# Smaller weight pieces, kept split parts and four row tiles in each sum over experts: a two-layer hybrid decoder trunk

## The chip, the cores and the metric

The kernel runs on one core of a Trainium2 chip. The core has five engines with instruction streams of their own: TensorE (PE, matrix multiplications into PSUM), VectorE (DVE), ScalarE (ACT), GpSimd (POOL) and SyncE (SP), which here issues every DMA. The metric is the time of the device in microseconds (us); lower is better. One execution was taken by the hardware profiler, and all rows of the trace come from it.

## The reference

Two layers over 1040 tokens (16 meta tokens and 1024 real ones; 112 padding places are masked) of width 1024, in float32. Each layer mixes tokens and then applies a product-key expert network:

```
for i in range(DEPTH):                                   # 2
    h = h + hybrid_mixer(rms_norm(h, attn_norm[i]), w_in[i], ..., w_out[i])
    h = h + peer_ffn(rms_norm(h, ffn_norm[i]), peer_w_q[i], peer_sub_keys[i], peer_u[i], peer_v[i])
return rms_norm(h[:, BLOCK:], final_norm)

# peer_ffn: 8 heads, 64 x 64 = 4096 experts, 16 chosen for each head
q = (xt @ wq).reshape(t, 8, 2, 128)
s = einsum('thpd,hpnd->thpn', q, sub_keys)               # scores of the two halves of a key
...                                                      # top 16 of the pairs, softmax g, expert idx
h_all = xt @ u.T                                         # (tokens, 4096): the hidden rows
a = gelu(take_along_axis(h_all, idx)) * g
w = zeros((t, 4096)).at[..., idx].add(a)
out = w @ v                                              # the sum over experts
```

The mixer projects the tokens to some 2300 columns, runs a sliding window attention, a stick-breaking attention and a gated linear attention on them, norms the three, and multiplies by `w_out`.

## The kernel before, in words

Activations are held transposed, 8 row tiles of 128 (`KT`) by tokens, and the tokens are cut in four quarters of 272, 256, 256 and 256 columns. The residual stream lies in DRAM.

**High and low parts.** A float32 product is made of three products in a rounded format, float32r: each operand is split into a high part (rounded, by ACT) and a low part (the difference, by DVE or POOL), and PE computes high x high, high x low and low x high. For weights, `wtile` loads 128x1024 float32 into one of three buffers `wraw`, and `split` (L273, L280) writes `whi` and `wlo`, two buffers each. `split_on` sets which engine takes the low part: POOL alone, or POOL and DVE a half each. For the weights of the sum over experts the other operand, `G`, is split too, for each row of experts r: `ah` on ACT (L1179), `al` on DVE (L1180).

**Stages of a layer.**
- Mixer: for each quarter 18 weight tiles of projections (`proj_span`) and 8 of the output (`out_span`), each through `dense` (L309 to L316): one tile, 8 x 3 matmuls over the quarter's columns. Every weight tile is loaded and split again in each quarter. The attention of a quarter is interleaved with the projections of the next one. `make_m` folds the query weights and keys into matrices `m`, which go to DRAM, 8 tiles of 128x1024 in each layer.
- Experts, for the first two quarters (P) and then for the last two (Q): `scores` multiplies the normed tokens by `m`, one head pair c at a time; `route` (many small DVE operations) finds the top 16; `hidden` runs over 32 row tiles r of u, each with 8 x 3 matmuls, and writes gelu of the result to `G`; `gates` builds the gate of every expert for 16 tokens at a time and multiplies it in; `values` sums over r = 0 to 31 with v, some row tiles d of the output at a time, accumulating in PSUM banks.
- In layer 0, the quarters of P are 272 and 256 columns wide, and a matmul takes one of them; in layer 1 the meta tokens are left out of P, both are 256 wide, and one matmul takes 512 columns. Q is 512 wide in both layers. `values` for P in layer 0 makes passes of 3, 3 and 2 row tiles (two banks for each row tile, six banks in all), and for P in layer 1 and Q in layer 0 two passes of 4. In the last layer, Q is summed in four passes: each quarter, row tiles 0 to 3, then each quarter, row tiles 4 to 7, with the final norm of P's quarters between the first two.
- During `values` of P the work of Q's first steps is spread over the loop: two `apply`, four `scores` (one after each 24 units of nd, from L1304 on), and the steps of `route`, `BUD * nd` of their estimated us after each r.

**Order.** The program is written as a stream of tile operations; a planner with a simulated timeline orders each engine's instructions, and each engine then runs its own in order, waiting on semaphores. SP too: a DMA that waits holds up those behind it.

Of the kernel before, what the change touches and what calls it, by code (L numbers as in the profile page):

```python
# [12 lines left out]
F32 = mybir.dt.float32  # L13
F32R = mybir.dt.float32r
# [28 lines left out]
class Span:  # L43
    """Token columns c0..c1 with their matmul chunks and 128-token tiles."""
# [18 lines left out]
def tile_trunk(ctx, tc, h0, w_pk, wgate, w2, glab, w_out, wqT, keysT, u_pk, v_w, sinks,  # L63
# [8 lines left out]
    # Buffers are views of two tiles, at fixed places: those of the mixer and of the experts share the room.  # L72
    # One tile has the operands rounded to float32r, the other the rest.
# [23 lines left out]
    g0 = lay(1, [("wraw", 1024, 3), ("ht", 528, 3), ("nsq", 528, 1), ("ndg", 128, 2), ("acc", T, 1), ("nms", 8, 2),  # L97
# [74 lines left out]
    set_rings(d=(0, 1), o=(2,), a=(3, 4, 5, 6, 7), h=(0, 1, 6, 7), g=(2, 3), v=(4, 5, 6, 7, 2, 3))  # L172

    # ---------------------------------------------------------------- constants
# [63 lines left out]
    # residual stream, transposed, in DRAM; sums of squares of each version on chip  # L238
# [25 lines left out]
    # ---------------------------------------------------------------- helpers  # L264
# [17 lines left out]
    def wload(src, n=1024):  # L282
        raw = sb([128, n], F32, "wraw", 4)
        SP.dma_start(raw, src)
        return raw

    def wtile(src, n=1024):
        raw = wload(src, n)
        n = raw.shape[1]
        hi = sb([128, n], F32R, "whi", 3)  # L290
        lo = sb([128, n], F32R, "wlo", 3)
        split(raw, hi, lo)
        return hi, lo

    class Rows:
        """Row tiles of hi and lo parts, in two halves."""
# [12 lines left out]
    def dense(wsrc, x, sp, xo=0):  # L309
        wh, wl = wtile(wsrc)  # L310
        ps = ps1("d")[:, 0:sp.w]
        for k in range(KT):
            ks = slice(k * 128, (k + 1) * 128)
# [5 lines left out]
    def rstd(ver, sp, sqk=None):  # L319
        """Reciprocal root mean square of each token of a quarter, on every partition."""  # L320
# [27 lines left out]
    def apply(ver, sp, g, x, rb, ks=range(KT), src=None):  # L348
        """Normed rows of a quarter, hi and lo."""
# [11 lines left out]
    # ---------------------------------------------------------------- folded product keys  # L361
    m_scr = [[dram.tile([128, KT * 128], F32, name=f"m{l}_{i}", tag=f"m{l}_{i}") for i in range(8)]
             for l in range(DEPTH)]

    def make_m(l, i):
        wq = [wload(wqT[l, 2 * i + e]) for e in range(2)]
        kt = sb([128, 2, 64], F32, "kt", 2)
        SP.dma_start(kt, keysT[l][:, 2 * i:2 * i + 2, :])
        for half in range(2):
            ps = ps1("d")  # L370
            for e in range(2):
                PE.matmul(ps[64 * e:64 * e + 64, :], kt[:, e, :], wq[e][:, half * 512:half * 512 + 512],
                          start=True, stop=True)
# [7 lines left out]
            SP.dma_start(m_scr[l][i][:, half * 512:half * 512 + 512], mk)  # L381

    # ---------------------------------------------------------------- attention
# [20 lines left out]
    def proj_span(l, L, sp, x):  # L404
        """Projections of a span: two blocks, with the meta tokens before them in the first."""
# [5 lines left out]
        def proj(g):  # L411
            return dense(w_pk[l, g], x, sp)
# [46 lines left out]
        # gate: hi and lo parts of the 16 columns stacked on 32 output rows  # L459
# [30 lines left out]
    def gla_setup(l, L, A):  # L490
# [4 lines left out]
        # GLA factors over the two blocks of the span; every exponent is at most zero  # L495
# [45 lines left out]
    def post(l, A, src, k0, nk, b0, nb, m, t0, gate=False, scale=1.0, eps=None):  # L541
        """Per-head norm, gain or gate of rows k0.. of the mix: src [128, (block, row tile, token)]; hi and lo parts."""
# [38 lines left out]
    def swa(l, L, A, n):  # L581
        """Sliding window of block n (-1: the meta tokens): query rows, keys of this block and the one before."""
# [8 lines left out]
        for kh in range(2):  # L591
# [34 lines left out]
            # the sum of the exponentials only scales its row, which the norm takes out but for its epsilon  # L626
# [29 lines left out]
    def sbreak(l, L, A, n, oT):  # L656
        """Stick breaking of block n: product of (1 - beta) over the newer keys, times beta."""
# [15 lines left out]
        for p in range(2):  # L673
            carry = [None, None]
            om = None
            for ci in range(nch):
# [4 lines left out]
                for e in range(2):  # L681
# [7 lines left out]
                    # t = tanh(z / 2): beta = (1 + t) / 2, 1 - beta = (1 - t) / 2  # L689
# [54 lines left out]
    def gla(l, L, A, n, outp=True):  # L744
        """Gated linear attention of block n: chunks of 8 directly, rectangles between them, state before."""
# [670 lines left out]
```

## Time and profile before

| | |
|---|---|
| median of 3 runs | 3486.05 us (3485.88 to 3488.12) |
| profiled execution, span from first to last instruction | 3482.2 us; a time of its own is not listed, and the span is 3.85 us under the median |
| mean granted TensorE clock | 0.956 of full speed |
| busy: PE, DVE, POOL, ACT | 3189.6, 2656.3, 1658.7, 1506.9 us |
| DMA | 373.16 MB, mean 107 GB/s |

Busy times overlap: each engine has its own. A stage's length less PE's busy time in it is the time in which PE had nothing to multiply. In the rows below, "x" is a count, "<-" in a group's tail names what ended the idle time before it, and L280 is line 280 of the kernel.

### The profile page before, as it was taken

How to read it: one execution, taken by the hardware profiler on the slowest of the kernel's cores; microseconds unless marked ns; L12 is line 12 of the kernel's file. 1: busy time of each engine (PE TensorE's matmuls, PEld its weight loads, DVE VectorE, ACT ScalarE, POOL GpSimd, SP SyncE). 2: the span in 40 equal slices, each digit the busy share in tenths (PEclk: the TensorE clock that was granted, in tenths of full speed). 3: DMA queues.
4: the chain of work that ended last, by engine and by line, in shares of the span. 5: the costliest groups of instructions: out<-in, count | busy, mean ns of one | idle time of the engine just before them, and what ended most of it. 6: DMA issues, size and time to landing. Idle time of an engine off the chain costs nothing. (4 is left out here: it accounts for less than half of the span.)

```text
span 3482.2 us, 62244 instructions
## 1 busy us (share of the span) xinstructions
PE 3189.6 (92%) x22843; PEld 2680.2 (77%) x22843; DVE 2656.3 (76%) x7223; ACT 1506.9 (43%) x3181; POOL 1658.7 (48%) x1179
## 2 busy tenths in 40 slices
PE   8999999988889988999899999999879899989899
PEld 7677887688879877887776878876768677767798
DVE  4667667599896799786356676676899868988887
ACT  4555545432234444334344545454323333333465
POOL 4435454343484433574432454543435534446655
PEclk9899998999899999999999999999989999999999
DMA  5434442342113322223433353333422133322454
GB/s 151 132 96 160 117 127 81 116 143 68 56 47 101 97 87 76 79 73 101 133 102 128 104 166 115 117 103 114 149 73 66 62 108 118 105 71 73 126 188 160
DMA packets 180948, 373.16 MB, mean 107 GB/s; under 512 B 18257, under 2 KB 79777, under 8 KB 180641
## 3 DMA queue, kind: packets, MB, share of 16 engines
q1 hardware_dynamic: 180640, 369.18, 33.7%
q8 instruction: 179, 2.93, 0.3%
q14 instruction: 129, 1.05, 0.1%
HBM read 341.71 MB, written 27.39 MB: 106 GB/s over the span
## 5 line engine op out<-in xcount | busy, mean ns | idle before, releaser
L280 POOL TENSOR_TENSOR arena_r<-arena,arena_r 128x512 fp32r<-128x512 f32 (+2 forms) x540 | 1108.1, 2053 | 1266.5 <-ACT arena_r L273 1217.4
L273 ACT ACTIVATE arena_r<-arena 128x1024 fp32r<-128x1024 f32 (+1 forms) x550 | 574.6, 1045 | 719.0 <-issue 207.3
L1186 PE MATMUL b<-arena_r 128*128 128x256 f32 (+2 forms) x4608 | 774.0, 326 | 73.1 <-DVE arena_r L1180 61.6
L1086 PE MATMUL b<-arena_r 128*128 128x512 f32 (+2 forms) x3840 | 792.4, 366 | 35.8 <-ACT arena_r L273 21.9
L1186 PEld LDWEIGHTS b<-arena_r 128*128 128x128 f32 x4608 | 667.4, 192 | 173.7 <-DVE arena_r L1180 94.5
L1086 PEld LDWEIGHTS b<-arena_r 128*128 128x128 f32 x3840 | 649.6, 199 | 141.4 <-ACT arena_r L273 24.9
L315 PE MATMUL b<-arena_r 128*128 128x256 f32 (+1 forms) x4992 | 696.0, 294 | 25.6 <-DVE arena L337 4.9
L315 PEld LDWEIGHTS b<-arena_r 128*128 128x128 f32 x4992 | 639.6, 195 | 62.1 <-issue 25.4
L1180 DVE TENSOR_TENSOR arena_r<-arena,arena_r 128x256 fp32r<-128x256 f32 (+2 forms) x448 | 399.9, 912 | 120.9 <-ACT arena_r L1179 119.5
L280 DVE TENSOR_TENSOR arena_r<-arena,arena_r 128x512 fp32r<-128x512 f32 (+1 forms) x290 | 234.7, 809 | 259.3 <-ACT arena_r L273 256.6
L1179 ACT ACTIVATE arena_r<-arena 128x256 fp32r<-128x256 f32 (+2 forms) x448 | 208.2, 474 | 170.4 <-PE b L1186 154.0
L1124 DVE TENSOR_TENSOR arena<-arena 128x2048 f16<-128x2048 f16 x129 | 200.3, 1555 | 40.0 <-PE b L1141 40.0
L1159 POOL TENSOR_TENSOR arena<-arena 128x352 f32<-128x352 f32 (+21 forms) x129 | 156.8, 1227 | 63.8 <-DVE arena L1147 34.7
L966 PE MATMUL b<-arena_r 128*128 128x256 f32 (+1 forms) x544 | 159.0, 295 | 16.3 <-POOL arena_r L280 9.4
L967 PE MATMUL b<-arena_r 128*128 128x256 f32 (+1 forms) x544 | 158.2, 294 | 7.8 <-DVE arena_r L359 7.8
L965 PE MATMUL b<-arena_r 128*128 128x256 f32 (+1 forms) x544 | 154.7, 293 | 2.6 <-ACT arena_r L358 1.1
L696 DVE TENSOR_TENSOR_SCAN arena<-arena,zf 128x272 f32<-128x272 f32 (+6 forms) x116 | 120.5, 1045 | 32.5 <-ACT arena L691 31.6
L256 POOL TENSOR_TENSOR arena<-arena 128x256 f32<-128x256 f32 (+2 forms) x105 | 99.8, 950 | 81.9 <-ACT arena L255 81.8
L1128 DVE TENSOR_TENSOR arena<-arena 128x512 f16<-128x512 f16 x129 | 127.4, 988 | 8.1 <-PE b L1153 7.8
L1146 ACT ACTIVATE arena<-b 128x64 f32<-128x64 f32 (+27 forms) x256 | 62.8, 283 | 160.5 <-DVE arena L1147 130.2
L1093 POOL TENSOR_TENSOR arena<-arena 128x272 f32<-128x272 f32 (+25 forms) x86 | 96.1, 1122 | 75.6 <-DVE arena L1147 48.0
L1129 DVE TENSOR_TENSOR arena<-arena 128x512 f16<-128x512 f16 x129 | 129.6, 1005 | 0.0
(277 smaller groups left out, 4613.7 us busy)
## 6 DMA issues: line engine op xcount, KB each, us to landing
arena<-in_w_pk_dram SPq DMA_DIRECT2D x144, 512.0 KB, 3.6
arena<-in_v_w_dram SPq DMA_DIRECT2D x136, 512.0 KB, 3.4
arena<-in_u_pk_dram SPq DMA_DIRECT2D x128, 512.0 KB, 3.5
arena<-in_w_out_dram SPq DMA_DIRECT2D x64, 512.0 KB, 3.7
arena<-m SPq DMA_DIRECT2D x92, 256.0 KB, 3.5
arena<-h SPq DMA_DIRECT2D x136, 128.0 KB, 2.3
arena<-in_wqT_dram SPq DMA_DIRECT2D x32, 512.0 KB, 3.8
arena<-in_v_w_dram SPq DMA_DIRECT2D x32, 384.0 KB, 3.1
```

Source lines behind the costliest of these rows:

```text
L273: ACT.activation(hi, src, AF.Copy)
L280: e.tensor_tensor(lo[:, a:b], src[:, a:b], hi[:, a:b].bitcast(F32), op=ALU.subtract)
L315: PE.matmul(ps, wt[:, ks], x.at(low, k, xo, sp.w), start=(k == 0 and i == 0), stop=(k == KT - 1 and i == 2))
L965: PE.matmul(ps[0:m, 0:256], yv(half, 0, k, oo, m), mh, start=(k == 0), stop=False)
L966: PE.matmul(ps[0:m, 0:256], yv(half, 0, k, oo, m), ml, start=False, stop=False)
L967: PE.matmul(ps[0:m, 0:256], yv(half, 1, k, oo, m), mh, start=False, stop=(k == KT - 1))
L1086: PE.matmul(ps, wt[:, ks], yv(h, low, k, 0, w // 2 if h is None else w), start=(k == 0 and i == 0), stop=(k == KT - 1 and i == 2))
L1124: DVE.tensor_tensor(Lh, iotaM.unsqueeze(1).to_broadcast([128, 4, 128, 4]), v4(P.mT, 128), op=ALU.is_equal)
L1159: POOL.tensor_tensor(G[:, 0:n, t0:t0 + 16], gt[:, 0:n], G[:, 0:n, t0:t0 + 16], op=ALU.mult)
L1179: ACT.activation(ah, G[:, r, o:o + w], AF.Copy)
L1180: last = DVE.tensor_tensor(al, G[:, r, o:o + w], ah.bitcast(F32), op=ALU.subtract)
L1186: PE.matmul(ps, wt[:, co:co + 128], pr[low], start=(r == 0 and i == 0), stop=(r == 31 and i == 2))
```

## The change

A weight piece is now 128x512: `wraw` has four buffers of 512, `whi` and `wlo` five each. At its first use a piece is split and, under a key, its low part (and for the projections and the output its high part too) is stored in DRAM. At later uses of the same key the low part is loaded from there; the high part is loaded too where it was kept, and converted again from the loaded weights where it was not. Keys: the projections and outputs of all four quarters, the scores' matrices (halves of P, and Q), u and v for P and Q. `values` always takes four row tiles at a time; where the two quarters are not merged, the second one's sums lie two to a bank. In the last layer Q's first four row tiles are summed for both quarters at once; the other four, a quarter at a time, under no key. `m` is stored as four matrices of 128x2048 per layer, one for each head pair, and `scores` puts two token tiles in one bank. `make_m` loads halves.

```diff
-    r0 = lay(0, [("whi", 1024, 2), ("wlo", 1024, 2), ("ah", 272, 4), ("al", 272, 4)], 0)
+    r0 = lay(0, [("whi", 512, 5), ("wlo", 512, 5), ("ah", 272, 4), ("al", 272, 4)], 0)
...
-    g0 = lay(1, [("wraw", 1024, 3), ("ht", 528, 3), ("nsq", 528, 1), ("ndg", 128, 2), ("acc", T, 1), ("nms", 8, 2),
+    g0 = lay(1, [("wraw", 512, 4), ("ht", 528, 3), ("nsq", 528, 1), ("ndg", 128, 2), ("acc", T, 1), ("nms", 8, 2),
...
+    kept = {}
+    def keep(name, part):
+        t = dram.tile([128, 512], F32, name=name, tag=name)
+        SP.dma_start(t, part.bitcast(F32))
+        return t
+    def wpiece(src, key=None, both=False):
+        hi = sb([128, 512], F32R, "whi")
+        lo = sb([128, 512], F32R, "wlo")
+        if key not in kept:
+            split(wload(src), hi, lo)
+            if key is not None:
+                kept[key] = (keep(f"{key}h", hi) if both else None, keep(f"{key}l", lo))
+            return hi, lo
+        kh, kl = kept[key]
+        if kh is None:
+            ACT.activation(hi, wload(src), AF.Copy)
+        else:
+            SP.dma_start(hi.bitcast(F32), kh)
+        SP.dma_start(lo.bitcast(F32), kl)
+        return hi, lo
...
-    def dense(wsrc, x, sp, xo=0):
-        wh, wl = wtile(wsrc)
+    def dense(wsrc, x, sp, key, xo=0):
...
+            if k % 4 == 0:
+                wh, wl = wpiece(wsrc[:, k * 128:(k + 4) * 128], f"{key}_{k // 4}", True)
...
     def scores(l, P, c, halves, ring):
+        pairs = [own[i:i + 2] for i in range(0, len(own), 2)]
+        bks = [ps1(ring) for _ in pairs]
+        for kq in range(4):
+            wh, wl = wpiece(m_scr[l][c][:, kq * 512:(kq + 1) * 512], f"m{l}_{c}_{kq}")
...
     def hidden(l, P, G, lo, hi, ring, cst=None, end=32):
-            wh, wl = wtile(u_pk[l, r])
...
+                if k % 4 == 0:
+                    wh, wl = wpiece(u_pk[l, r][:, k * 128:(k + 4) * 128], f"u{l}_{r}_{k // 4}")
...
-    def values_steps(l, P, G, halves, d0, nd, hs=None):
+    def values_steps(l, P, G, halves, d0, hs=None, reuse=True):
...
+        for i, (h, o, w) in enumerate(cs):
+            for d in range(4):
+                if i and d % 2:
+                    accs[d][i] = (bank[:, 256:256 + w], False, True)
+                else:
+                    bank = ps1("v")
+                    accs[d][i] = (bank[:, 0:w], True, not i)
+        for r in range(32):
+            wh, wl = wpiece(v_w[l][:, r, d0 * 128:d0 * 128 + 512], f"v{l}_{r}_{d0}" if reuse else None)
...
-        for d, nd in ((0, 4), (4, 4)) if P.merge else ((0, 3), (3, 3), (6, 2)):
-            for last, whole in values_steps(l, P, G, (0, 1), d, nd):
+        for d in (0, 4):
+            for last in values_steps(l, P, G, (0, 1), d):
...
-                if whole and work and step >= EVERY:
+                if work and step >= EVERY:
...
-                    left = BUD * nd
+                    left = BUD * 4
...
-        values(l, Q, G, (0,), 0, 4, hs)
+        values(l, Q, G, (0, 1), 0, hs)
...
-        values(l, Q, G, (1,), 0, 4, hs)
         for half, (o, sp) in enumerate(Q.parts):
-            values(l, Q, G, (half,), 4, 4, hs)
+            values(l, Q, G, (half,), 4, hs, False)
```

## Rows read from the trace of the kernel before

**Rows 1.** The page's part 1: busy us (share of the span) x instructions.

```profile
PE 3189.6 (92%) x22843; PEld 2680.2 (77%) x22843; DVE 2656.3 (76%) x7223; ACT 1506.9 (43%) x3181; POOL 1658.7 (48%) x1179
```

**Rows 2.** Stretches: start:end, length; PE, PEld, DVE, ACT, POOL busy; clock; DMA share, GB/s.

```profile
100.00:640.00 540.00, 517.34 (x3893) 398.34 (x3892) 364.98 (x738) 284.16 (x666) 250.03 (x225) 0.95 0.39 123
1050.00:1350.00 300.00, 264.65 (x2013) 254.32 (x2012) 249.61 (x1030) 135.21 (x291) 118.96 (x65) 0.97 0.30 93
1350.00:1595.00 245.00, 231.09 (x1346) 186.83 (x1347) 208.01 (x413) 92.17 (x239) 149.38 (x102) 0.96 0.25 78
1850.00:2440.00 590.00, 567.50 (x4246) 443.05 (x4245) 403.49 (x862) 306.33 (x687) 257.34 (x230) 0.96 0.39 123
2500.00:2770.00 270.00, 233.50 (x1812) 187.93 (x1810) 255.99 (x742) 84.39 (x159) 140.04 (x80) 0.93 0.22 69
2770.00:3030.00 260.00, 235.94 (x1153) 188.28 (x1154) 206.41 (x842) 92.83 (x141) 102.27 (x43) 0.99 0.33 106
3030.00:3265.00 235.00, 218.59 (x1292) 177.35 (x1291) 209.24 (x455) 87.39 (x227) 144.14 (x89) 0.96 0.25 79
3265.00:3482.00 217.00, 198.77 (x1631) 195.73 (x1629) 174.71 (x242) 119.06 (x213) 123.92 (x67) 0.96 0.55 175
```

**Rows 3.** The timeline, PE: start us, length us, line, operation, shape, count.

```profile
1799.78 34.47 PE L1186 MATMUL b<-arena_r 128*128 128x512 f32 x146
3338.24 27.03 PE L1186 MATMUL b<-arena_r 128*128 128x256 f32 x228
```

**Rows 4.** The timeline around 2803 us: DVE and POOL.

```profile
2800.35 0.69 DVE L1180 TENSOR_TENSOR arena_r<-arena,arena_r 128x512 fp32r<-128x512 f32 x1
2803.11 2.41 POOL L280 TENSOR_TENSOR arena_r<-arena,arena_r 128x1024 fp32r<-128x1024 f32 x1 [4.05 <-ACT arena_r L273]
2803.59 3.08 DVE L1180 TENSOR_TENSOR arena_r<-arena,arena_r 128x512 fp32r<-128x512 f32 x2 [2.55 <-ACT arena_r L1179]
```

**Rows 5.** Groups by shape, DVE and ACT: busy us, mean ns | idle before.

```profile
L1180 DVE TENSOR_TENSOR arena_r<-arena,arena_r 128x512 fp32r<-128x512 f32 x128 | 157.1, 1237 | 77.4 <-ACT arena_r L1179 76.5
L1179 ACT ACTIVATE arena_r<-arena 128x512 fp32r<-128x512 f32 x128 | 79.5, 622 | 78.5 <-PE b L1186 77.9 <-POOL arena L1159 0.6
L273 ACT ACTIVATE arena_r<-arena 128x1024 fp32r<-128x1024 f32 x518 | 547.6, 1058 | 694.9 <-issue 201.5 <-PE b L1186 173.7 <-PE b L315 107.2
```

**Rows 6.** Waits of PE, whole span: us in total, times, longest us.

```profile
PE b L1186 <- DVE arena_r L1180: 61.6, 71, 2.4
PE b L1110 <- DVE arena L1019: 19.1, 2, 12.4
```

**Rows 7.** POOL's splits: the page's group, then the 512-column shape alone.

```profile
L280 POOL TENSOR_TENSOR arena_r<-arena,arena_r 128x512 fp32r<-128x512 f32 (+2 forms) x540 | 1108.1, 2053 | 1266.5 <-ACT arena_r L273 1217.4
L280 POOL TENSOR_TENSOR arena_r<-arena,arena_r 128x512 fp32r<-128x512 f32 x280 | 467.9, 1672 | 513.9 <-ACT arena_r L273 484.6 <-issue 26.8 <-DMA arena<-h 2.4
```

**Rows 8.** The stretch 1050 to 1350, L1180 alone: DVE busy us (count).

```profile
1050.00:1350.00 300.00, 127.04 (x185) 0.97 0.30 93
```

**Rows 9.** Groups by shape, 1350 to 1595 us: PE's gate matmuls.

```profile
L1141 PE MATMUL b<-arena 128*128 128x64 f16 x512 | 35.7, 242 | 2.0 <-DVE arena L1147 2.0
```

**Rows 10.** DMA issues: count, KB each, median us from issue to landing.

```profile
arena<-m SPq DMA_DIRECT2D x92, 256.0 KB, 3.5
arena<-in_w_pk_dram SPq DMA_DIRECT2D x144, 512.0 KB, 3.6
```

**Rows 11.** Waits of SP, whole span: us in total, times, longest us.

```profile
SPq L354 <- DVE arena_r L359: 100.6, 50, 7.7
SPq L246 <- DMA h<-arena: 83.7, 49, 4.1
SPq L261 <- DVE arena L260: 64.8, 37, 8.5
```

**Rows 12.** Stretches of the first quarters' projections, columns as in rows 2.

```profile
25.00:100.00 75.00, 66.02 (x485) 60.18 (x484) 35.58 (x91) 36.35 (x81) 33.76 (x30) 0.95 0.46 138
1675.00:1760.00 85.00, 74.37 (x502) 67.78 (x502) 25.70 (x39) 30.42 (x47) 38.36 (x22) 0.98 0.46 144
```

More of the change, by code (lines that the diff above doesn't have):

```diff
@@ L370, in make_m @@
             ps = ps1("d")
+            wq = [wload(wqT[l, 2 * i + e][:, half * 512:half * 512 + 512]) for e in range(2)]
             for e in range(2):
-                PE.matmul(ps[64 * e:64 * e + 64, :], kt[:, e, :], wq[e][:, half * 512:half * 512 + 512],
-                          start=True, stop=True)
+                PE.matmul(ps[64 * e:64 * e + 64, :], kt[:, e, :], wq[e], start=True, stop=True)
             mt = sb([128, 512], F32, "ht")
@@ L952, in scores @@
[L952 removed]
         if P.s[c] is None:
[L954 removed]
+            P.s[c] = sb([128, P.ns, len(sp.tiles), 4, 64], F32, "s")[:, c % P.ns]
             if sp.meta:
                 POOL.memset(P.s[c][:, 0], 0.0)
[L957 to L968 removed]
+        own = [(j, o, m) for j, (o, m) in enumerate(sp.tiles) if (1 if o >= P.parts[1][0] else 0) in halves]
@@ new lines, in scores @@
+        own.sort(key=lambda t: -t[2])
+        pairs = [own[i:i + 2] for i in range(0, len(own), 2)]
+        bks = [ps1(ring) for _ in pairs]
+        for kq in range(4):
+            wh, wl = wpiece(m_scr[l][c][:, kq * 512:(kq + 1) * 512], f"m{l}_{c}_{kq}")
+            for bk, pair in zip(bks, pairs):
+                for e, (j, o, m) in enumerate(pair):
+                    half = 1 if o >= P.parts[1][0] else 0
+                    oo = o - P.parts[half][0]
+                    ps = bk[0:m, e * 256:e * 256 + 256]
+                    for kk in range(2):
+                        k = 2 * kq + kk
+                        for i, (low, wt) in enumerate(((0, wh), (0, wl), (1, wh))):
+                            PE.matmul(ps, yv(half, low, k, oo, m), wt[:, kk * 256:kk * 256 + 256],
+                                      start=(k == 0 and i == 0 and e == 0),
+                                      stop=(k == KT - 1 and i == 2 and e == len(pair) - 1))
@@ L970, in route @@
+        for bk, pair in zip(bks, pairs):
+            for e, (j, o, m) in enumerate(pair):
+                ACT.activation(P.s[c][0:m, j], bk[0:m, e * 256:e * 256 + 256].rearrange("p (a n) -> p a n", a=4), AF.Copy)
     def route(*args):
@@ new lines, in values_steps @@
+        accs = [[None] * len(cs) for d in range(4)]
+        for i, (h, o, w) in enumerate(cs):
[7 more added lines that the diff above has]
+            wh, wl = wpiece(v_w[l][:, r, d0 * 128:d0 * 128 + 512], f"v{l}_{r}_{d0}" if reuse else None)
+            parts = []
+            for h, o, w in cs:
+                tg = "2" if w > 272 else ""
+                ah = sb([128, w], F32R, "ah" + tg)
+                al = sb([128, w], F32R, "al" + tg)
+                ACT.activation(ah, G[:, r, o:o + w], AF.Copy)
+                last = DVE.tensor_tensor(al, G[:, r, o:o + w], ah.bitcast(F32), op=ALU.subtract)
+                parts.append((ah, al))
+            for d in range(4):
+                for i, (wt, low) in enumerate(((wh, 0), (wh, 1), (wl, 0))):
+                    for (ps, opens, closes), pr in zip(accs[d], parts):
+                        PE.matmul(ps, wt[:, d * 128:d * 128 + 128], pr[low], start=(opens and r == 0 and i == 0),
+                                  stop=(closes and r == 31 and i == 2))
+            yield last.ins
@@ L1191, in values_steps @@
+        for d in range(4):
+            for (ps, _, _), (h, o, w) in zip(accs[d], cs):
                 sp = P.sp if h is None else P.parts[h][1]
```

85 lines of the change are left out of this document (17 added, 68 removed).

## The prediction

> **What bounds the kernel now.** I read the page first: TensorE (PE) is busy 92% of 3482.2 us, VectorE (DVE) 76, GpSimd (POOL) 48 and ScalarE (ACT) 43% [rows 1]. So work that leaves ACT, POOL and DVE is worth only what it now costs PE in waits. The stretches by stage come next [rows 2]: I set PE's busy time against a stage's length and then look at who else is full. In the two mixers (100 to 640, 1850 to 2440) PE lacks 23 us each. In layer 0's first sum over experts (1050 to 1350) it lacks 35 of 300 us, with DVE busy 250. In the hidden rows of the first two quarters (2500 to 2770, layer 1) DVE is busy 256 of 270: there the routing and the gates are the limit, not weights. The rate that PE reaches when nothing waits comes from the timeline [rows 3]: 34.47 us for 146 matmuls of 512 columns, 0.236 us each, and 27.03 for 228 of 256 columns, 0.1186 each. Two of 256 cost what one of 512 costs.
>
> Why a split of weights costs PE anything is seen in three rows side by side [rows 4]: two conversions on DVE (L1180) take 3.08 us together while one POOL split of 2.41 us runs, where one alone takes 0.69. DVE's two-operand work stands still behind POOL's. Its mean shows it too: 1237 ns for 512 columns [rows 5]. PE waited 61.6 us for L1180 in all [rows 6].
>
> **The change, part by part.** The profiled span is 3482.2 us, 3.9 under the median of the runs, 3486.05; the sum is made on the span and 3.9 is added.
>
> *Bytes and splits.* Counted in pieces of 128x512 (0.262 MB), from the loops. First uses: 104 of the projections and of the output, 128 of the hidden rows, 128 of the sums, 32 of the scores, and 64 in the last pass that keep nothing: 456 full splits, the work of 228 old tiles where there are 550. Reuses: 312 that take both parts from DRAM, and 284 (128, 96, 60) that take the low part and convert the high one. ACT then has 740 conversions of 0.622 us [rows 5], 460 us for some 575. POOL's 1108 us [rows 7] fall to about 500. Written: 208 + 128 + 128 + 32 = 496 pieces, 130 MB more; read: 312 + 128 + 96 + 60 - 32 = 564 pieces, 148 MB more. That makes 651 MB for 373. At 0.55 of the DMA engines' time 175 GB/s moved in the last stage [rows 2], so full is about 318 GB/s, and the mean after is 191: 60%. The average has room; bursts are looked at below.
>
> *Sum over experts, first half, layer 0: 300 us, taken at -40.* Passes of 3, 3 and 2 row tiles become 4 and 4, so 64 of the 192 pairs of conversions go: at 127.04/185 = 0.69 us [rows 8] that is 44 us of DVE's 250. PE needs 1536 x 0.1186 x 264/256 + 384 x 0.1186 (scores) = 233 us; below that it can't go (-67). The nearest row is layer 1's same stage, which already runs 4 and 4: 260 us [rows 2]. The 16 columns more add 768 x 0.0085 = 7. So 267, or -33, and -7 for the effect of the next paragraph. Upper end 0.
>
> *The same sum, layer 1: 260 us, taken at -12.* A split of 1024 columns on POOL (2.41 us) becomes two, one for each row of experts. A conversion that meets one now needs 0.62 (ACT) + 2.41 + 0.69 = 3.7 us against 12 x 0.236 = 2.83 us of matmuls; with half the split (1.2, or 1.67 as the 512-column splits take now [rows 7]) 2.5 to 3.0. Most of that wait goes. Ends -35 (PE's need is 225) and +5.
>
> *Hidden rows, second half: 245 and 235 us, taken at 0 and -10.* Here POOL's splits vanish, and DVE's gates run free of them. PE needs 768 x 0.236 = 181 and 36 of gates [rows 9], 217. What is late next is the end of the routing: in layer 1 PE stood 12.4 us for it [rows 6], since four row tiles give fewer row steps and so fewer turns of routing in the loop (46 with some 1.4 of its estimated us each, where layer 0 now has 40 of 1.4 and 32 of 0.7). Layer 0 gets that stall: -8 and +8. Ends -46 and +12 for both.
>
> *Sums of the second half: layer 0 0, the last stage (217 us) -6.* One pass over 512 columns for two of 256 saves PE nothing (0.236 against 2 x 0.1186), but 32 conversions. Ends -25 and +15.
>
> *Mixers: 540 and 590 us, taken at -16 together.* 156 of 208 weight tiles lose their splits: 165 us of ACT and 261 of POOL (1058 and 1672 ns each [rows 5, 7]), all beside PE. What it can give is PE's 45 us of idle time, so -45 is one end. The other is the loads. A piece lasts 12 x 0.1186 = 1.42 us in a run of matmuls; with five buffers it is asked for 5.7 us ahead, and 256 KB land in 3.5 us [rows 10]: 2.2 us to spare, where three raw and two split tiles gave 14 us. SP issues in order, and behind each store or load that waits the next pieces wait too. The three largest such waits that are not for a weight buffer have 249 us in 136 times, 1.83 each, up to 8.5 [rows 11]. If they are spread as exponential, the part over 2.2 us is 0.55 each, 75 us, about half of it in the mixers: +40.
>
> *Each layer's first quarter: +16.* A piece then moves 0.79 MB, 2.5 us at 318 GB/s, for 12 x 0.126 = 1.5 us of matmuls. 36 pieces take 89 us where the stretches have 75 and 85 us [rows 12]; the stores hold buffers, so part of it reaches PE: +12 and +4. Ends 0 and +30. SP also waits there for the low part before it can store it, but the raw load behind waited for that same split before.
>
> *Hidden rows, first half: +5.* The splits stay, in two instructions of up to 1672 ns for one of 2.4 us, beside a full DVE. Ends -15 and +30. *Scores: -4*, ends -10 and +10.
>
> *Clock: -10.* The mean granted clock is below 1 in every stage [rows 2], 0.93 where PE lacks most; fewer waits mean fewer stretches at 1.2 GHz. Ends -50 and 0.
>
> Sum: -40 - 12 + 0 - 10 - 6 - 16 + 16 + 5 - 4 - 10 = -77. 3482.2 - 77 + 3.9 = 3409 us.
>
> One rule speaks against the change. In the trace 256 KB land in 3.5 and 512 KB in 3.6 us [rows 10]: a smaller transfer is hardly sooner there. The Trainium skill (DMA: Bandwidth & Descriptors, Bandwidth) says to batch transfers to 1 MiB for 75% of the peak, and its section on the anatomy of one DMA gives each a fixed 2 us (measured on another queue) beside the bytes. By that, one after another, the four pieces of a tile would take 10.4 us, an estimate from that page, and the mixers would grow by several hundred us; whether transfers overlap in flight decides it, and the 175 GB/s of the last stage speak for overlap. The form of it that rows support is the second rival.
>
> **Rivals.**
> 1. *PE starves behind SP's queue (slower).* Place: the mixers and output projections, with 5.7 us of lead for 14. For it: the waits of [rows 11]. Against: attention work lies between dense tiles, some 78 tiles in 540 us (104 less 18 before and 8 after), so the mean lead is twice that. If half of the 249 us reach PE, +125 in place of -16, and with the other gains (-61) the time is 3550; it decides against the change from about 61 us, a quarter of those waits. I take 3530 as its middle.
> 2. *DMA rate in dense runs.* A reused tile moves 1.05 MB, 3.3 us at 318 GB/s, for 24 x 0.1186 = 2.85 us. If all 156 run at that rate: +70 for -16, and the first quarters +30 for +16: 3409 + 86 + 14 = 3509; 3460 if half is hidden under attention work.
> 3. *Only the layer 0 sum pays.* ACT and POOL were never PE's limit, so the rest is given back: 3486 - 40 + 10 = 3456.
> 4. *POOL's lock was the hidden cost everywhere.* With DVE free in all reuse stages PE comes near its need: -67, -35, -46, -45, clock -40, and +11 for the rest: -222 or 3264; with three quarters of it 3320, its middle.
> 5. *Parts are kept but seldom read.* The second pass of the last sums splits again although its low parts were stored; were it so elsewhere, only the stores and the smaller pieces would be new: 3500.
>
> **How the numbers follow.** Forecast 0.53 (own range 3360 to 3440), rival 4 0.13, rival 3 0.15, rival 2 0.07, rival 1 0.10, rival 5 0.02. The range takes in rival 3, half of 4 and most of 2: 3320 to 3490, with some 0.19 left out. A change under 0.2%, 7 us, can't be told from none. Faster: 0.50 of the forecast, 0.13, 0.14 and 0.03 of rival 2, together 0.80. Slower: 0.10, 0.02 and 0.03 of rival 2, 0.15. The same: 0.05.
>
> **What would show it.** Right: POOL under 600 us busy; the layer 0 sum at 250 to 275 us; L1180's mean under 1000 ns at 512 columns; 600 to 680 MB moved; PE's idle time in the mixers no larger. Wrong: PE waits on DMA of kept parts in the mixers (rivals 1 and 2), a first quarter over 100 us, or a stall of over 20 us before the slots of the second half.

## The result, and the profile after

| | median us | ratio to before, 95% interval |
|---|---|---|
| before | 3487.09 | |
| after | 3389.60 | 0.9718 [0.9698, 0.9738] |

The change makes the kernel 97 us faster. 3409 was predicted. The profiled execution after has a span of 3391.3 us, 90.9 less than that of before. Part 1 of its page, the DMA total and queue q1 of part 3:

```profile
PE 3157.8 (93%) x22459; PEld 2647.5 (78%) x22459; DVE 2172.3 (64%) x7020; ACT 1381.1 (41%) x3278; POOL 1091.0 (32%) x1092
...
DMA packets 397222, 651.27 MB, mean 192 GB/s; under 512 B 43536, under 2 KB 109152, under 8 KB 396896
...
q1 hardware_dynamic: 396896, 647.16, 59.3%
```

Against [rows 1], POOL is busy 568 us less, DVE 484 and ACT 126. The span falls by 90.9 us, 32 of them PE's busy time and 59 its idle time, so most of what left the other engines was never on the path. The bytes are the 651 MB that were counted.

The stretches after, bounds set at PE's milestones, the ends of a stage's last matmul (layer 0: mixer, sum of the first half, hidden rows of the second; layer 1: mixer, hidden rows and sum of the first half, hidden rows and sum of the second). Columns as in [rows 2]:

```profile
115.00:723.00 608.00, 579.30 (x4416) 451.45 (x4417) 327.42 (x915) 246.97 (x648) 151.63 (x193) 0.96 0.66 210
1062.00:1320.00 258.00, 242.62 (x1922) 236.78 (x1922) 194.83 (x931) 105.39 (x249) 89.11 (x68) 0.99 0.59 183
1320.00:1532.00 212.00, 211.70 (x1290) 172.27 (x1288) 145.80 (x436) 96.25 (x265) 59.40 (x68) 1.00 0.53 168
1799.00:2411.00 612.00, 579.68 (x4324) 451.15 (x4324) 336.40 (x932) 249.87 (x637) 146.48 (x174) 0.94 0.65 207
2452.00:2709.00 257.00, 228.19 (x1713) 183.62 (x1711) 234.64 (x740) 87.16 (x179) 141.62 (x104) 0.91 0.41 138
2709.00:2969.00 260.00, 239.51 (x1264) 196.19 (x1264) 199.36 (x891) 103.12 (x197) 101.99 (x72) 0.96 0.61 192
2969.00:3177.00 208.00, 208.00 (x1262) 170.28 (x1261) 144.13 (x409) 92.70 (x251) 56.67 (x55) 1.00 0.52 165
3177.00:3380.00 203.00, 194.48 (x1244) 174.16 (x1243) 122.26 (x211) 102.39 (x215) 69.33 (x73) 0.97 0.59 178
```

And before, three of these stages between the same milestones (sum of layer 0's first half, then the hidden rows of the second half in layer 0 and in layer 1):

```profile
1065.00:1366.00 301.00, 261.46 (x1950) 249.12 (x1950) 261.84 (x1089) 135.93 (x290) 117.38 (x62) 0.96 0.30 93
1366.00:1587.00 221.00, 213.59 (x1275) 173.16 (x1273) 185.89 (x347) 83.51 (x225) 136.66 (x95) 0.97 0.24 76
3030.00:3266.00 236.00, 219.59 (x1296) 178.17 (x1295) 209.96 (x459) 88.07 (x231) 144.70 (x90) 0.96 0.25 78
```

In the third and seventh stretch after, PE never lacks work and its clock is 1.00. In the mixers (first and fourth stretch) it still lacks 29 and 32 us, though POOL, DVE and ACT each do far less there. The two mixers before, between the same milestones:

```profile
101.00:712.00 611.00, 583.64 (x4404) 452.93 (x4402) 415.05 (x956) 314.27 (x718) 278.68 (x257) 0.96 0.39 122
1860.00:2453.00 593.00, 570.00 (x4306) 447.31 (x4305) 412.69 (x952) 310.00 (x693) 264.73 (x237) 0.96 0.40 126
```

The groups after that answer to [rows 5, 7], by shape but for POOL's, which is the page's: conversions of gated activations on DVE (L1204, before L1180), high parts made again on ACT for kept low ones (L307), POOL's splits (L280).

```profile
L1204 DVE TENSOR_TENSOR arena_r<-arena,arena_r 128x512 fp32r<-128x512 f32 x160 | 131.9, 828 | 192.1 <-ACT arena_r L1203 191.6
...
L307 ACT ACTIVATE arena_r<-arena 128x512 fp32r<-128x512 f32 x284 | 178.5, 631 | 327.4 <-PE b L1209 130.5 <-PE b L1104 90.7 <-issue 62.0
```

```profile
L280 POOL TENSOR_TENSOR arena_r<-arena,arena_r 128x512 fp32r<-128x512 f32 (+1 forms) x453 | 561.0, 1246 | 867.9 <-ACT arena_r L273 813.9
```

The first wait of PE's list over the whole span, and the first two of SP's, as [rows 6, 11]:

```profile
PE b L1209 <- DVE arena_r L1204: 24.7, 35, 1.8
```

```profile
SPq L292 <- POOL arena_r L280: 682.5, 285, 17.3
SPq L309 <- PE b L334: 394.8, 217, 15.1
```

PE's wait for the conversions falls from 61.6 to 24.7 us. New on SP: the stores of kept parts (L292) wait 682.5 us for POOL's splits, and the loads of kept high parts (L309) 394.8 us for a buffer that PE still reads.

### The profile page after: what moved, and what is told of

The parts are those of the page before. It is cut to its first block, busy times and chain, and to the rows that moved or that the text cites. A ratio compares the mean times of both kernels' runs of the same rounds, so it can differ in the third digit from the quotient of the medians.

```text
span 3391.3 us, 64331 instructions
## 1 busy us (share of the span) xinstructions
PE 3157.8 (93%) x22459; PEld 2647.5 (78%) x22459; DVE 2172.3 (64%) x7020; ACT 1381.1 (41%) x3278; POOL 1091.0 (32%) x1092
## 4 chain that ended last, share of the span: by engine, by line
PE 59%; DVE 23%; DMA 6%; ACT 2%; issue 2%; POOL 1%; SPq 0%; POOLq 0%; DVEq 0%; ACTq 0%
PE b L1209 14%; PE b L1104 13%; PE b L334 12%; PE b L980 4%; DVE arena L1142 2%; DMA arena<-h 2%; PE b L704 2%; DVE arena_r L1204 2%; PE b L1159 2%; DVE arena L998 2%; DVE arena L999 2%; PE b L758 1%; DVE arena L1001 1%; PE b L619 1%; DVE arena L1147 1%
## 5 line engine op out<-in xcount | busy, mean ns | idle before, releaser
L280 POOL TENSOR_TENSOR arena_r<-arena,arena_r 128x512 fp32r<-128x512 f32 (+1 forms) x453 | 561.0, 1246 | 867.9 <-ACT arena_r L273 813.9
L1104 PE MATMUL b<-arena_r 128*128 128x512 f32 (+2 forms) x3840 | 782.3, 363 | 23.4 <-ACT arena L1113 13.5
L1209 PE MATMUL b<-arena_r 128*128 128x512 f32 (+2 forms) x4224 | 755.4, 337 | 36.5 <-DVE arena_r L1204 24.7
L334 PE MATMUL b<-arena_r 128*128 128x256 f32 (+1 forms) x4992 | 694.6, 293 | 33.8 <-ACT arena_r L273 10.2
L273 ACT ACTIVATE arena_r<-arena 128x512 fp32r<-128x512 f32 x456 | 285.1, 629 | 472.4 <-PE b L1104 124.4
L1204 DVE TENSOR_TENSOR arena_r<-arena,arena_r 128x512 fp32r<-128x512 f32 (+2 forms) x352 | 260.5, 751 | 230.9 <-ACT arena_r L1203 230.1
L307 ACT ACTIVATE arena_r<-arena 128x512 fp32r<-128x512 f32 x284 | 178.5, 631 | 327.4 <-PE b L1209 130.5
L980 PE MATMUL b<-arena_r 128*128 128x256 f32 (+1 forms) x1632 | 220.6, 291 | 15.3 <-DMA arena_r<-m_0l 5.3
L980 PEld LDWEIGHTS b<-arena_r 128*128 128x128 f32 (+1 forms) x1632 | 205.4, 190 | 27.9 <-DMA arena_r<-m_0l 7.3
L1177 POOL TENSOR_TENSOR arena<-arena 128x448 f32<-128x448 f32 (+20 forms) x129 | 144.2, 1123 | 150.8 <-DVE arena L1165 115.4
L1203 ACT ACTIVATE arena_r<-arena 128x512 fp32r<-128x512 f32 (+2 forms) x352 | 171.7, 502 | 25.2 <-PE b L1209 23.6
L280 DVE TENSOR_TENSOR arena_r<-arena,arena_r 128x256 fp32r<-128x256 f32 (+1 forms) x187 | 101.0, 546 | 92.1 <-ACT arena_r L273 71.2
L716 DVE TENSOR_TENSOR_SCAN arena<-arena,zf 128x384 f32<-128x384 f32 (+6 forms) x116 | 104.3, 903 | 79.0 <-ACT arena L711 77.8
```

Source lines behind the costliest of these rows:

```text
L273: ACT.activation(hi, src, AF.Copy)
L280: e.tensor_tensor(lo[:, a:b], src[:, a:b], hi[:, a:b].bitcast(F32), op=ALU.subtract)
L307: ACT.activation(hi, wload(src), AF.Copy)
L334: PE.matmul(ps, wt[:, ks], x.at(low, k, xo, sp.w), start=(k == 0 and i == 0), stop=(k == KT - 1 and i == 2))
L716: DVE.tensor_tensor_scan(keep[0:m, 0:wd][:, ::-1], keep[0:m, 0:wd][:, ::-1], zf[0:m, 0:1].to_broadcast([m, wd]), keep[0:m, wd:wd + 1], op0 ...
L980: PE.matmul(ps, yv(half, low, k, oo, m), wt[:, kk * 256:kk * 256 + 256], start=(k == 0 and i == 0 and e == 0), stop=(k == KT - 1 and i == ...
```

## The experiments

Each run's ratio is to the kernel before, timed beside it on the same chip; whole times of kernels that were not timed together are compared by these ratios. Stage lengths are from PE's milestones in one trace of each kernel. Two kernels below that are alike up to the end of layer 1's mixer take 603.5 and 597.1 us in it, so a few us in one stage of one trace prove nothing.

**Four row tiles alone** (the kernel before):

```
-  for d, nd in ((0, 4), (4, 4)) if P.merge else ((0, 3), (3, 3), (6, 2)):
+  for d, nd in ((0, 4), (4, 4)):          # and two 256-column sums to a bank
...
```

> The kernel before with one thing of the change: layer 0's first sum over experts in two passes of four row tiles, the second quarter's sums two to a bank; weights in 1024-column tiles, split at every use. Theory (the gain there is 64 fewer pairs of conversions on VectorE, 0.69 us each, and needs no kept parts): the time from the last hidden row of the first half to the last sum, 300.4 us before and 258.6 with the whole change, comes to 262 to 270 and the kernel to about 3450 to 3455 (ratio 0.989 to 0.991). Rival (that stage was held by POOL's long splits, and only the smaller pieces opened it): 285 to 300 there, 3475 to 3487 in all. Both expect the next 20 to 40 us to lose up to 10 to the routing left over.

Measured: 3475.43 us, 0.9971 [0.9958, 0.9985]. The sum takes 276.4 us (before 300.4), and the hidden rows behind it 238.6 (before 221.1).

```profile
1059.00:1335.00 276.00, 249.93 (x1921) 242.76 (x1920) 213.61 (x916) 102.58 (x209) 104.09 (x48) 0.96 0.30 95
1335.00:1574.00 239.00, 222.80 (x1300) 179.02 (x1299) 208.89 (x455) 88.61 (x234) 148.24 (x102) 0.96 0.26 80
```

DVE loses 48 us in the sum and gains 23 in the next stage: the routing that had its turns in the longer sum is left over. Of the 24 us 18 are lost again in the hidden rows, half of that as idle time of PE (7.4 to 16.2 us).

**Nothing kept** (the kernel after; every use splits):

```
-  if key is not None:
+  if False:
```

> The changed kernel with nothing kept: every piece of 512 columns is split at every use, no part is stored or read back. Theory (of the 97 us some 42 come from the four row tiles and some 55 from reuse, which takes POOL's splits away from VectorE in the second halves): 3440 to 3460; hidden rows of the second half back from 212 and 208 to 220 and 228 us; first quarter 103 us instead of 115; layer 1's mixer 595 instead of 612. Rival (small pieces and deeper rings do it, and keeping is for nothing): 3385 to 3405.

Measured: 3415.87 us, 0.9797 [0.9774, 0.9821]. The time lies between theory and rival. Some 70 of the 97 us come without keeping a byte (the kernel moves 365 MB); keeping is worth some 27. The hidden rows of the second halves go back to 223.0 and 226.1 us, as the theory had it, and the first quarter to 98.3, but layer 1's mixer takes 604.2 us and not 595: part of what it lost comes with the small pieces.

**Pieces alone** (nothing kept, and 3, 3 and 2 row tiles again in layer 0's first sum):

```
-  for d in (0, 4):
+  for d, nd in ((0, 4), (4, 4)) if P.merge else ((0, 3), (3, 3), (6, 2)):
...
```

> The kernel after with nothing kept and the layer-0 sum of the first half taken 3, 3 and 2 row tiles at a time again: what is left of the change is the 512-column pieces, the deeper rings of parts, the regrouped scores and the merged last passes. Nothing-kept with four tiles took 3416, four tiles alone in the old pieces gave back 24 us in the sum and lost 18 right behind it. Theory (four tiles are the larger part of the sum's gain, the pieces let it show): the sum takes 275 to 285 us, 3435 to 3450 in all. Rival (the small pieces do it by themselves, since a part is ready twice as soon): the sum stays at 255 to 262 and the whole at 3415 to 3425.

Measured: 3444.99 us, 0.9898 [0.9869, 0.9928]. The whole time is the theory's; the sum takes 287.5 us, 2.5 over its range, the hidden rows behind it 209.3. So the pieces with their rings (and the regrouped scores and merged last pass, which weren't taken apart) give 1.0%, and four tiles on top of them another 1.0% (to 0.9797). In the sum itself: 12.9 us the pieces, 32.6 the tiles, of which 13.7 come back behind it. The two stages together take 521.5 us before, 496.8 with the pieces, 477.9 with the tiles too and 470.6 in the kernel after, so over both stages the pieces, with what came along with them, give more than the tiles. Both shorten PE's wait for the conversions, 61.6 us before [rows 6]: with four tiles alone, with pieces alone, with both and nothing kept it is

```profile
PE b L1193 <- DVE arena_r L1187: 41.1, 51, 2.7
```

```profile
PE b L1216 <- DVE arena_r L1210: 38.8, 40, 4.0
```

```profile
PE b L1209 <- DVE arena_r L1204: 23.9, 19, 4.0
```

and 24.7 in the kernel after. Keeping the parts adds nothing to this.

**Hidden weights not kept** (the kernel after, key None for u):

```
-  wh, wl = wpiece(u_pk[l, r][:, k * 128:(k + 4) * 128], f"u{l}_{r}_{k // 4}")
+  wh, wl = wpiece(u_pk[l, r][:, k * 128:(k + 4) * 128], None)
```

> The changed kernel, but the hidden rows keep nothing: u is split again for the second half; the rest as changed. Theory (the second half's hidden rows gained because POOL's splits no longer hold up VectorE's gates): the two stages go from 212 and 208 us back to 220 to 235, with L1142 and its neighbours on VectorE longer; the first half's hidden rows stay within 4 us of 302 and 257; in all 3410 to 3425. Rival (they gained from elsewhere, as routing that ended sooner): 205 to 215 each, 3375 to 3392 in all, since 34 MB are no longer written.

Measured: 3415.47 us, 0.9801 [0.978, 0.9823]. The hidden rows of the second halves take 222.4 and 224.9 us beside 212.0 and 208.3. Layer 1's stage of this kernel, then the timeline's row of the first transpose of the slots in it (L1128), of this kernel and of the kernel after:

```profile
2969.00:3194.00 225.00, 211.70 (x1247) 172.36 (x1246) 186.80 (x415) 88.38 (x246) 142.59 (x113) 0.96 0.26 86
```

```profile
3010.58 0.47 PE L1128 MATMUL b<-ident,arena 128*128 128x128 f32 x1 [11.41 <-DVE arena L1036]
```

```profile
2999.09 0.27 PE L1128 MATMUL b<-ident,arena 128*128 128x128 f32 x1
```

Both stages begin at 2969 us. With the splits PE stands 11.4 us for the last step of the routing (L1036); without them it is ready before PE asks. What made it late is seen in the same DVE operations, from 2949 us to the transpose: lines by shape, busy us and mean ns, with the splits and then without.

```profile
L1070 DVE TENSOR_TENSOR arena<-arena 128x2048 f16<-128x2048 f16 x3 | 5.6, 1877 | 0.0
L1083 DVE COPY arena<-arena 128x128 f16<-128x128 f16 x1 | 1.5, 1508 | 0.0
L1082 DVE SCALAR_TENSOR_TENSOR arena<-arena 128x128 f16<-128x128 f16 x1 | 1.4, 1353 | 0.0
```

```profile
L1070 DVE TENSOR_TENSOR arena<-arena 128x2048 f16<-128x2048 f16 x3 | 3.6, 1216 | 0.0
L1083 DVE COPY arena<-arena 128x128 f16<-128x128 f16 x1 | 0.5, 466 | 0.0
L1082 DVE SCALAR_TENSOR_TENSOR arena<-arena 128x128 f16<-128x128 f16 x1 | 0.3, 285 | 0.0
```

POOL is busy 142.6 us in the one stage and 56.7 in the other. Operation by operation, DVE's routing is 1.7 us behind the kernel after at 2973 us, 8.7 behind at 2990 and 12.7 at the end. In both stretches POOL was splitting, four times in a row at the end of each:

```profile
2985.34 5.36 POOL L280 TENSOR_TENSOR arena_r<-arena,arena_r 128x512 fp32r<-128x512 f32 x4
3002.50 6.71 POOL L280 TENSOR_TENSOR arena_r<-arena,arena_r 128x512 fp32r<-128x512 f32 x4 [11.80 <-ACT arena_r L273]
```

DVE stands behind POOL even in small operations, as it did in [rows 4]. The Trainium skill (SBUF — State Buffer, Who interferes with whom) says that DVE and GpSimd share a port pair as a lock held for the whole instruction; the 285 ns operation that takes 1353 beside the splits agrees.

**Only the hidden weights kept** (the kernel after):

```
-  if key is not None:
+  if key is not None and key[0] == "u":
...
```

> The kernel after with only the low parts of the hidden layer's weights kept; projections, scores and sums make theirs from raw pieces each time. The kernel that keeps these and the scores' and sums' parts took 3370. Theory (what pays is a POOL that is quiet while the routing's tail runs on VectorE, in the second halves' hidden layer; keeping the sums' parts is worth little): 3368 to 3382, hidden of the second halves 208 to 214 us. Rival (the sums' kept parts pay as much, in the second halves' sums): 3385 to 3400, with the sums of the second halves 4 to 10 us longer.

Measured: 3392.67 us, 0.9742 [0.9716, 0.9768]: the rival's time. The hidden rows take 212 and 209 us as expected, though no other parts are kept: together with the preceding run, which keeps all but these, that settles where the second halves' hidden rows gain. Beside the next kernel, which also keeps parts for the sums and scores, 0.7% is missing. The sums of the second halves are 5.7 and 3.4 us longer than there, as the rival had it, but 15 us lie in layer 0's first hidden rows and the mixers are 5 and 2 us shorter, so I don't put it to one stage.

**Projections and output not kept** (the kernel after, in `dense`):

```
-  wh, wl = wpiece(wsrc[:, k * 128:(k + 4) * 128], f"{key}_{k // 4}", True)
+  wh, wl = wpiece(wsrc[:, k * 128:(k + 4) * 128], None)
```

> The changed kernel, but the projections and the output keep nothing: their pieces are split in each quarter; hidden rows, sums and scores still keep their low parts. Theory (in the mixers engines beside TensorE had room, so keeping there gains nothing and the extra 54 MB written and 82 MB read cost): first quarter of layer 0 back to 101 to 104 us (115 with the change), layer 1's mixer to 595 (612), layer 0's about 608; in all 3355 to 3375. Rival (freeing ACT, POOL and VectorE in the mixers is part of the gain): 3400 to 3420, with TensorE's idle time in both mixers up by 10 us or more.

Measured: 3370.01 us, 0.9672 [0.9645, 0.9699], the theory's time, and faster than the change (the intervals just touch). The largest class of kept parts costs some 16 us net. The stages follow the theory only in part. The first quarter falls to 97.2 us and layer 1's first projections from 73.9 to 68.1, but layer 0's mixer takes 621.0 us (608.4 in the kernel after, and expected) with PE idle for 39.9 in place of 28.7, as the rival had it for that mixer, and layer 1's 604.8 (595 expected).

**Low part of these alone** (`both` left False there, so that the high part is made again by ACT):

```
-  wh, wl = wpiece(wsrc[:, k * 128:(k + 4) * 128], f"{key}_{k // 4}", True)
+  wh, wl = wpiece(wsrc[:, k * 128:(k + 4) * 128], f"{key}_{k // 4}")
```

> The kernel after with only the low part of the projections' and output's weights kept; the high part is made from the raw piece again at each use, by ScalarE. Half of the stores in the first quarters go away. Theory (the price of the kept projections is the stores and the queue they stand in: each store waits for its split, and the next piece's load is behind it): the first quarter falls from 115 to 104 to 109 us, layer 1's first projections from 74 to 70 to 72, the mixers stay within 5 us; 3375 to 3385 in all. Rival (the price is the reads in the mixers, or ScalarE then becomes late there): 3390 to 3405, first quarter no better than 112.

Measured: 3359.07 us, 0.9646 [0.9619, 0.9674], past the theory's own range (3375 to 3385). First quarter 100.8 us, layer 1's first projections 66.8, its mixer 594.4; layer 0's mixer takes 613.7.

**High parts stored but not read** (the kernel after, in `wpiece`):

```
-  if kh is None:
+  if True:
```

> The kernel after with the high parts of the projections' and output's weights still stored, but made again from the raw piece at each use: the stores of the kernel after with the reads of the kernel that keeps low parts only (3359, first quarter 100.8, layer 1's mixer 594 us, beside 3390, 114.6 and 612). Theory (the first quarter's price is the bytes of the stores, the mixer's is the kept high part's load, which may not go out before a buffer of the ring of parts is free): first quarter 112 to 116, layer 1's mixer 592 to 600, 3365 to 3378 in all. Rival (all of the price is the stores): mixer of layer 1 605 to 613, 3382 to 3395.

Measured: 3382.81 us, 0.9715 [0.9698, 0.9732]. That is the kernel after again, and the whole time lies in the rival's range. The kernel with low parts alone reads the same bytes (a raw piece in place of each kept high part) and is 0.7% faster; what it leaves out is the 104 stores of high parts, 27 MB. So their price is the stores, not the loads. The first quarter takes 113.1 us, 12.3 more than with low parts alone. Layer 1's mixer, 605.4, is in the rival's range too, but it scatters by as much from trace to trace.

**Stores from ScalarE's queue** (in `keep`):

```
-  SP.dma_start(t, part.bitcast(F32))
+  ACT.dma_start(t, part.bitcast(F32))
```

> The kernel after with the stores of the kept parts issued from ScalarE's instruction stream in place of SyncE's, so that a store which waits for its split no longer holds back the loads behind it in SP's queue; the same bytes and pieces. Theory (head of line on SP, whose stores waited 683 us on the splits on POOL): first quarter 98 to 105, hidden of layer 0's first half 293 to 298, 3365 to 3375 in all. Rival (the bytes themselves or the splits are the price): within 5 us of 3390. Second rival (ScalarE now waits for POOL at each store, and its own high parts come late): slower than 3400.

Measured: 3365.04 us, 0.966 [0.9635, 0.9686], the time that the theory gave, but not at its places: the first quarter still takes 110.3 us, and the hidden rows of layer 0's first half 302.4. The sums of the first halves fall to 253.5 and 251.3 us (258.6 and 259.9 in the kernel after). Why the move helps there is not shown. SP waits for POOL's splits as long as before, now at the raw loads (L284), which need a buffer that a split still reads; and the stores have a DMA queue of their own, q10, beside the loads. Either the order or the second queue can be the cause. SP's first wait, and q10 in part 3 of the page:

```profile
SPq L284 <- POOL arena_r L280: 818.7, 339, 15.8
```

```profile
q10 hardware_dynamic: 71424, 130.06, 10.1%
```

In the first quarter the bytes stand out. The stretch of 25 to 100 us (as [rows 12]) of this kernel, of the kernel after (with layer 1's, 1631 to 1705) and of the one that stores low parts alone:

```profile
25.00:100.00 75.00, 65.54 (x464) 58.87 (x463) 37.49 (x114) 38.50 (x103) 35.15 (x46) 0.93 0.95 329
```

```profile
25.00:100.00 75.00, 62.62 (x428) 56.17 (x427) 31.90 (x81) 33.37 (x82) 31.74 (x42) 0.91 0.88 303
1631.00:1705.00 74.00, 64.02 (x458) 58.77 (x456) 22.55 (x43) 28.40 (x58) 33.53 (x34) 0.98 1.00 357
```

```profile
25.00:100.00 75.00, 67.01 (x492) 62.36 (x491) 36.55 (x114) 39.13 (x101) 35.35 (x45) 0.93 0.78 256
```

With the stores off SP the DMA engines are 95% busy there; with fewer bytes they are 78% busy and the stage is 10 us shorter. In layer 1's first quarter (second row of the kernel after) they are full at 357 GB/s.

**Both edits together:**

> Both of the edits that helped by themselves: only the low parts of the projections' and output's weights kept (alone 3359), and the stores issued from ScalarE's stream (alone 3365, beside 3390 of the kernel after). Theory (two prices: bytes in the first quarter and in the mixers' reads, and the store's place in SP's queue in the sums, worth 5 and 9 us there): they add in part, 3340 to 3352. Rival (both shorten the same stalls): 3355 to 3365.

Measured: 3352.99 us, 0.9628 [0.961, 0.9645], between theory and rival, and not told apart from low parts alone (0.9646). So the move to ScalarE's queue shows in the whole time once, not twice, though the first halves' sums fall again (252.6 and 251.6 us, beside 260.8 and 258.6 with low parts alone). It has the lowest median of all, 129 us under the kernel before that was timed beside it.

**Unread parts not stored** (both edits, and 32 low parts of layer 1's sum never written):

```
-  if key is not None:
+  if key is not None and not (key.startswith("v1_") and key.endswith("_4")):
```

> The kernel with low parts only and stores on ScalarE's queue, and the 32 low parts of layer 1's sum over row tiles 4 to 7 not stored, since nothing reads them (8.4 MB less written in a stage of 260 us). Theory (off SP's queue a store costs nothing outside the first quarter): within 4 us of the kernel with both edits. Rival (the stores' bytes still count in the sums): 5 to 10 us faster, layer 1's first sum shorter by as much.

Measured: 3356.41 us, 0.9638 [0.962, 0.9655]: no difference that can be told, as the theory had it.

**Rings of three** (the kernel after):

```
-  [("whi", 512, 5), ("wlo", 512, 5), ...
+  [("whi", 512, 3), ("wlo", 512, 3), ...
```

> The kernel after with rings of three buffers for the high and the low parts in place of five. Theory (a kept part's load starts only when a buffer of the ring is free, and five pieces are about 14 us of matmuls in the dense stages, so three are 8 us beside a transfer of 3 to 4 us that queues behind others): the mixers grow by 5 to 20 us each with waits of PE on the kept parts' DMA, 3400 to 3440 in all. Rival (a transfer lands well inside two pieces of work): within 6 us of 3390.

Measured: 3400.49 us, 0.9761 [0.9739, 0.9783]: 0.4% slower than with five, just inside the theory's range. Both mixers are 8.6 us longer, but PE's waits there that are put down to kept parts stay small. Its largest in layer 1's mixer:

```profile
PE b L334 <- DMA arena_r<-o_0l: 3.3, 5, 1.7
PE b L334 <- DMA arena_r<-o_1l: 2.0, 3, 1.2
```

Over the whole span PE's waits for kept parts do rise, from 15 to 37 us; the two largest are in the scores, not in the mixers' projections that the theory named:

```profile
PE b L980 <- DMA arena_r<-m_0l: 9.2, 5, 3.4
PE b L980 <- DMA arena_r<-m_1l: 6.3, 3, 2.4
```

Layer 1's hidden rows of the first half and its last sums came out 8 and 9 us shorter than with five, which neither theory explains.

## Why the prediction was right, and where not

| step | predicted us | profiles, after less before |
|---|---|---|
| layer 0 sum, first half | -40 | -41.8 |
| layer 1 sum, first half | -12 | -9.5 |
| first quarters | +16 | +13.4 and +0.9 |
| hidden rows, second halves | 0 and -10 | -9.1 and -27.7 |
| mixers | -16 | -2.0 and +19.5 |
| hidden rows, first halves | +5 | -4.8 and -3.6 |
| scores | -4 | -10.2 and -6.5 |
| sums, second halves | 0 and -6 | -7.7 and -1.8 |
| clock, by itself | -10 | inside the others (mean 0.956 before, 0.955 after) |
| sum | -77 | -90.9 |

That the sum came out within 14 us is partly luck: the mixers were 33 us dearer than taken and the second halves' hidden rows 27 us cheaper, and the two cancel.

- *Layer 0's sum* was right. -33 for the tiles and -7 for the pieces were written; 32.6 and 12.9 were measured with the pieces taken first (the tiles alone, in the old pieces, gave 24.0), and keeping cost 3.7 again. What was not carried through is that the tiles alone send the routing into the next stage (238.6 us).
- *Hidden rows of the second halves* were the mis-sized term, 27 us. The stall of 8 us that I added to layer 0 is real: with four tiles alone PE's idle time there goes from 7.4 to 16.2 us. It is 8.3 when only the hidden weights split, and 0.3 in the kernel after; in layer 1 it falls from 16.4 us to none, and most of the other 11 us there are matmuls at a granted clock of 1.00 for 0.96. I had counted that DVE's gates run free once POOL is quiet, and not that the routing's tail does too, so that the stall goes as well. The gates' own operations show DVE free, in the layer 1 stage: a 512-element product that took 1202 ns (L1128 before) takes 612 (L1146 after).

```profile
L1146 DVE TENSOR_TENSOR arena<-arena 128x512 f16<-128x512 f16 x32 | 19.6, 612 | 0.0
```

```profile
L1128 DVE TENSOR_TENSOR arena<-arena 128x512 f16<-128x512 f16 x32 | 38.5, 1202 | 0.0
```

- *Mixers* were wrong. I took a third of PE's 45 idle us back because ACT and POOL do less; idle time did not fall (27 and 23 us before, 29 and 32 after), with some 120 us less POOL work in each. Two things are mixed in this. With nothing kept the small pieces alone lengthen the mixers, to 617.7 and 604.3 us, with PE idle for 36 in each:

```profile
98.00:716.00 618.00, 581.94 (x4409) 453.87 (x4408) 412.73 (x1054) 329.43 (x804) 289.78 (x349) 0.95 0.39 121
1808.00:2413.00 605.00, 568.96 (x4307) 449.96 (x4306) 425.28 (x1076) 332.77 (x791) 286.35 (x328) 0.95 0.40 124
```

  In layer 0 that is a price of 7.3 us, and keeping takes 9.3 back (608.4); in layer 1 the price is 11.6 us. I had looked for such a price in waits for loads, and those are a few us. Where PE pays it is open: its waits in these mixers are many and small, the largest 6.9 us in all. Layer 1's +19.5 is not settled either: the kernel after and the one whose hidden weights split have the same instructions there and took 612.1 and 599.1 us, the last two kernels with stores from ACT, alike up to there, 603.5 and 597.1, from one profile each, so a good part of it is not the change's.
- *First quarters*: right in size and, in layer 0, in cause: without the stores it is 96 to 98 us. Of its 13.4 us 6.0 are PE's idle time, the rest mostly longer matmuls (granted clock 0.91 in 25 to 100 us, 0.95 before). Whether PE waits for the bytes themselves or for the buffers that a store holds was not taken apart. 318 GB/s as full was low; 357 are seen.
- *Hidden rows of the first halves, scores*: both better than taken. The hidden rows are inside their ends; the scores, -16.7 in all, are past theirs (-10). The nothing-kept kernel has the scores' gain already (37 and 42 us to the first hidden row, for 47 and 48).
- *Clock*: no gain by itself. It rose to 1.00 in the second halves' hidden rows and fell in layer 1's mixer (0.96 to 0.94) and in the first quarter.
- *Rivals.* PE's largest wait on a kept part in a mixer after, in layer 1, is

```profile
PE b L334 <- DMA arena_r<-o_1l: 3.5, 3, 1.7
```

  so rival 1 has no place there. But the stores on SP did cost: 0.6% came back when they left that queue, by its order or by the second queue, most of it outside the waits that I had named. Rival 2 holds in the first quarters alone. Rival 4's lock holds where POOL goes quiet beside DVE work that PE needs.
- The rule on batching (the Trainium skill, DMA: Bandwidth & Descriptors, Bandwidth), taken for transfers one after another, would have made the mixers several hundred us dearer, by the prediction's estimate. The 256 KB pieces moved 357 GB/s with the engines full, so overlap decided it. The Trainium skill (DMA: Bandwidth & Descriptors, Specifications) gives some 358 GB/s as the limit of one core's HBM access, half of what a pair shares. The 357 lie next to it, but no run here shows that this limit was what was full.
- Of what I said would show it: "POOL under 600 us busy" is wrong as written (1091); my working was of its splits, which fell to 561. The sum (258.6 us), the 512-column mean (828 ns; 1041 with nothing kept, so half of its fall is the pieces'), the bytes and the vanished stall hold. PE's idle time in the mixers was to be no larger; it is. The warning of a first quarter over 100 us came true (114.6).

## What to carry to other kernels

Count a kept result's bytes at the stage where it is stored: keeping pays where it silences an engine that blocks the one on the path, and costs where the stage's DMA is already near full. Store only what can't be made again by an idle engine. Try stores that wait for a slow producer on another queue than the loads: here it gave 0.6% once, and nothing that can be told in a second kernel. When a stage is shortened, look at what had its turns inside it.

## What the runs showed of the hardware

- With the stores issued from ScalarE in place of SP, and equal bytes, the time went from 0.9718 to 0.966 of before; with low parts alone stored, from 0.9646 to 0.9628, which can't be told apart. SP's waits for POOL's splits did not shrink by it (682.5 us at the stores before the move, 818.7 at the loads with it), so the reason is open.
- DMA engines at share 1.00 moved 357 GB/s, nearly all in pieces of 256 KB, loads and stores mixed.
- A DVE operation on 128x128 16-bit elements went from 285 to 1353 ns beside POOL's splits; even a copy of one operand went from 466 to 1508.
- TensorE's granted clock was 1.00 in the stretches of 208 and 212 us in which PE was never without work, and 0.91 in one of 257 us in which it lacked 29.
